# Second attention pass of a hybrid backbone block: one subtraction of the maps for both heads of a step

## The chip, the cores and the metric

The kernel runs on one core of a Trainium2 chip. The metric is the device time of one execution in microseconds; the median of three runs before the change is 3882.36 us (3880.23 to 3885.21).

## The reference

Two layers act on 2048 latent tokens and a prefix of 256 context tokens, each of width 1024. A layer normalises and modulates its input, projects it to 14 slices of 256 columns, runs four mixers side by side (a two-way RG-LRU, a two-way HGRN2, a Conformer convolution of 31 taps, differential attention), gates each with a SiLU, projects the concatenation back, normalises it and adds it, gated, to the stream. Everything is fp32. The change is in the attention. It has 4 heads, each with two softmax maps over the keys (2304 of them for a latent query, 256 for a context query):

```
s = einsum('bqhd,bkhd->bhqk', q, keys) * scale        # 8 maps, d = 32
p = softmax(s, axis=-1).reshape(b, 4, 2, q, k)
a = p[:, :, 0] - lam * p[:, :, 1]                      # difference of the two maps
o = einsum('bhqk,bkhe->bqhe', a, vals)                 # e = 64
y = rms_norm(o, norm_g) * (1 - lam_init)
```

## The kernel before, in words

The instructions of the whole program are traced in Python and a scheduler then orders them engine by engine. It simulates the engines in time: among the instructions whose inputs and buffers are free it takes the one that was traced first. `mix` interleaves generators in given proportions and thereby sets the traced order; `issue_after` puts an instruction behind another one on the same engine. The order on each engine, the DMA queues of SP and ScalarE among them, is fixed in the program.

A layer has four stages. `half0` and `half1` project the tokens, and find the maximum and the sum of every row of the maps (first pass of attention). `first` and `second` make the second pass, which recomputes the scores with the row's maximum and logarithm of the sum folded in as two more rows of the contraction, so that one exponential gives the finished probabilities.

The second pass (`attention`, `att_b`) runs over two pairs of heads and, for each pair, over blocks of 512 queries (in layer 0 also one of the 256 context queries). A block is a chain of steps, one for each 128 keys: 18 steps for latent queries, 2 for the context block; 148 steps in layer 0 and 144 in layer 1. In a step each of the two heads has two score products into a two-bank accumulator `sb` (two such buffers), one exponential on ScalarE from there into `pb`, and one VectorE operation (`scalar_tensor_tensor`) that subtracts the second map, times lambda, from the first. `values` multiplies the differences of both heads with V and accumulates into `po`, a single buffer of one bank, head 0 in partitions 0 to 63 and head 1 in 64 to 127. Those products are held back in the list `late` and issued two steps later, behind the first head's score products. A product in fp32 appears as two records in the trace. After the last key `head_norm` squares `po` on ScalarE, multiplies `po` by the gate on VectorE (the gate's tile comes by DMA), sums the squares with TensorE, takes the reciprocal root on GpSimd, spreads it with TensorE, multiplies and stores.

Beside the steps run, in `first` (the first 92 steps), the second half of the RG-LRU (`lru`: long VectorE scans, stores issued from ScalarE), the splitting of the output weights and in layer 0 the modulation of layer 1; in `second` (the rest) the output projection (`out_rows`, 128 tokens at a time) and the convolution (`conf`, 30 VectorE operations for each of two channel tiles, begun in `first`). `out_rows` keeps its result in `ot` (two buffers), adds the residual from `xt` (one buffer) and stores from ScalarE's queue; `xt` and `y` are loaded on SP.

Of the kernel before, what the change touches and what calls it, by code (L numbers as in the profile page):

```python
# [97 lines left out]
class _Kern:  # L98
# [232 lines left out]
    def layer(self, l):  # L331
        tc, dr = self.tc, self.dr
        last = l == DEPTH - 1
        self.S = S = {}
        for n in ("hq", "hff", "hkf", "hfb", "hkb", "g0", "g1", "g2", "g3", "cv", "qh", "ql", "kh", "kl"):
            S[n] = dr.tile([GW, T], F32, name=f"{n}_{l}")
        for n in ("hv", "av"):
            S[n] = dr.tile([T, GW], F32, name=f"{n}_{l}")
        S["y"] = dr.tile([D, T], F32, name=f"y_{l}")
        for n in ("lab", "lub", "lyf"):  # L340
            S[n] = dr.tile([GW, 1024], F32, name=f"{n}_{l}")
        for n, w in (("cu", 3), ("cg", 30)):
            S[n] = dr.tile([GW, w + 1024], F32, name=f"{n}_{l}")
        if not last:
            S["xn"] = dr.tile([T, D], F32, name=f"xn_{l}")
        a, z = ("left", "right") if l % 2 == 0 else ("right", "left")

        def pool(es, name, bufs, side=None, **k):
            return es.enter_context(tc.tile_pool(name=f"{name}{l}", bufs=bufs, side=side, reuse_waits="tile", **k))

        self.pool = pool
        halo = ExitStack()
        self.hb = pool(halo, "hB", 1, a)
        self.st = pool(halo, "st", 4, a)
        self.wp = pool(halo, "w", 2, a)
        self.keep = pool(halo, "keep", 1, a)
        self.carry = {}
        self.tanhs = []
        self.pend = None
        self.ready = set()  # L360
        self.normed = set()
        self.att_done = False
        self.parts = {}
        self.late = []
        self.steps = 0
        self.exp = None
        self.nz = {}
        self.mzd = {}

        self.X = self.hb.tile([P, 2, 4, D], F32, name="h3")  # L370
        self.prep_in(l, 1, self.X[:, 0])
        self.prep_in(l, 0, self.X[:, 1])
        self.w0 = [self.weights(l, 8, 0), self.weights(l, 7, 0)]
        if l == 0:
            with ExitStack() as es:
                pl = es.enter_context(tc.tile_pool(name="mod0", bufs=1, side=z, reuse_waits="tile"))
                pp = es.enter_context(tc.tile_pool(name="modp", bufs=3, space=PSUM, side="left", reuse_waits="tile"))
                mix([[self.modulations(0, 512, pl, 4, lambda: pp.tile([P, 512], F32, name="mps")), 1]])
                self.derived = [self.params(k, pl) for k in range(self.depth)]
        self.pr = self.derived[l]  # L380
        with ExitStack() as es:
            self.hx = pool(es, "hX", 1, z)
            self.m = self.mc = pool(es, "m0", 6, z)
            self.gt = pool(es, "gt0", 1, z)
            self.pre = pool(es, "pre0", 1, a)
            self.pj = pool(es, "pj0", 3, "left", space=PSUM)
            self.pq = pool(es, "pq0", 2, "left", space=PSUM)
            self.psA = pool(es, "psA0", 3, "right", space=PSUM)
            self.half0(l)
        with ExitStack() as es:  # L390
            self.pc = pool(es, "pc", 1, z)
            self.ap_ = self.hg = pool(es, "hg", 1, z)
            self.pj = pool(es, "pj1", 1, "left", space=PSUM)
            self.pq = self.pj
            self.psA = pool(es, "psA1", 4, "right", space=PSUM)
            self.psm = pool(es, "psm", 3, "right", space=PSUM)
            self.psn = lambda: self.psm.tile([P, 512], F32, name="pm")
            self.half1(l)
        halo.close()
        with ExitStack() as at:  # L400
            self.ap_ = pool(at, "at", 1, z)
            self.psB = pool(at, "psB", 1, "right", space=PSUM)
            self.psA = pool(at, "psA2", 1, "right", space=PSUM)
            self.psn = lambda: self.psA.tile([P, 512], F32, name="sa")
            self.mc = pool(at, "mc", 4, a)
            self.st = pool(at, "st1", 1, a)
            with ExitStack() as es:
                self.m = pool(es, "m1", 9, a)
                self.keep = pool(es, "keep1", 2, a)
                self.pq = pool(es, "pq1", 2, "left", space=PSUM)  # L410
                self.psc = lambda: self.pq.tile([P, 512], F32, name="pj")
                self.side = a
                self.first(l)
            self.psc = self.psn
            self.second(l, a)
        for k in [k for k in self.dbg if k.endswith(f"_{l}")]:
            self.nc.sync.dma_start(out=self.dbg[k], in_=S[k[:-2]])
        if not last:
            self.xprev = S["xn"]
# [324 lines left out]
    def first(self, l):  # L744
# [26 lines left out]
        with ExitStack() as es:  # L771
            pl = self.pool(es, "wout", 2, self.side)
            parts.append([self.out_weights(l, pl), 92])
            if l + 1 < self.depth:
                pl = self.pool(es, "mod", 1, self.side)
                parts.append([self.modulations(l + 1, P, pl, 2, lambda: self.pq.tile([P, 512], F32, name="pj")), 92])
            mix(parts)

    def second(self, l, side):
        with ExitStack() as es:  # L780
            for t in self.tanhs[-12:]:
                es.enter_context(self.tc.issue_after(t.ins))
            self.nc.scalar.preload_act_table_set("natural_log_exp_and_others")
        mix([[self.att, 148 - 92], [self.outp(l, side), 60], [self.convs, 30]])

    def attention(self, l):
# [3 lines left out]
        for i, (hp, b) in enumerate(todo):  # L790
            if b == self.qbs[0]:
                kv = {c: self.att_keys(l, hp, c) for c in KEYS}
            qst = q
            if i + 1 < len(todo):
                q = self.att_q(l, *todo[i + 1])
            yield from self.att_b(l, hp, b, kv, qst)
        while self.late:
            self.late.pop(0)()
        self.att_done = True
        self.steps = 999  # L800

    def lru(self, l, ct, u):
        nc, S, hf = self.nc, self.S, self.hf
# [334 lines left out]
    def att_b(self, l, hp, b, kv, qst):  # L1138
# [7 lines left out]
        def values(kt, cbs):  # L1146
# [6 lines left out]
            if kt < nk - 1:  # L1153
                return
            keep = hp == 1 and b == self.qbs[-1]
            rs = self.head_norm(l, po, n, self.pr["dg"], S["g3"], hp, t0, 768, keep)
            if hp == 1:
                self.ready.add(b)
            if keep:
                self.last_y = rs  # L1160

        for kt, (kst, V, ki) in enumerate(tiles):
            cbs = []
            for h in range(2):
                ps = self.psB.tile([P, 2, 512], F32, name="sb", bufs=2)
                for m in range(2):
# [1 line left out]
                        ps[:, m, :n], kst[:98, 2 * h + m, ki * P : (ki + 1) * P], qst[2 * h + m][:98, :n],  # L1168
                        start=True, stop=True,
                    )  # L1170
                pb = ap_.tile([P, 2, 512], F32, name="pb", bufs=5)
                self.exp = nc.scalar.activation(out=pb[:, :, :n], in_=ps[:, :, :n], func=AF.Exp)  # L1172
                cb = pb[:, 1, :]
                nc.vector.scalar_tensor_tensor(  # L1174
                    out=cb[:, :n], in0=cb[:, :n], scalar=self.pr["nlam"], in1=pb[:, 0, :n],
                    op0=ALU.mult, op1=ALU.add,
                )
                cbs.append(cb)
                if h == 0 and len(self.late) > 1:
                    with self.tc.issue_after(qk.ins):  # L1180
                        self.late.pop(0)()
            self.late.append(lambda kt=kt, cbs=cbs: values(kt, cbs))
            self.steps += 1
            yield

    def head_norm(self, l, po, n, g, gate, ct, t0, yoff, keep=False):

        nc, S, ap_ = self.nc, self.S, self.ap_
        sq = ap_.tile([P, 512], F32, name="nn", bufs=2)
        nc.scalar.activation(out=sq[:, :n], in_=po[:, :n], func=AF.Square)  # L1190
        rs = ap_.tile([P, 512], F32, name="nn", bufs=2)
        nc.sync.dma_start(out=rs[:, :n], in_=gate[ct * P : (ct + 1) * P, t0 : t0 + n])
        nc.vector.scalar_tensor_tensor(  # L1193
            out=rs[:, :n], in0=po[:, :n], scalar=g, in1=rs[:, :n], op0=ALU.mult, op1=ALU.mult
        )
# [293 lines left out]
    def out_rows(self, l, wp, yp, pp, wh, wl):  # L1489
# [3 lines left out]
        for b in self.qbs:  # L1493
# [12 lines left out]
            for q in range(n // P):  # L1506
# [9 lines left out]
                )  # L1516
                xt = yp.tile([P, D], F32, name="xt", bufs=1)
                nc.sync.dma_start(out=xt, in_=self.xsrc(l, t0 // P + q))
                t = yp.tile([P, D], F32, name="ot")
                ss = yp.tile([P, D // 512], F32, name="oss")  # L1520
                pss = {}

# [37 lines left out]
                for h in range(1, D // 512):  # L1560
                    nc.gpsimd.tensor_tensor(out=ss[:, 0:1], in0=ss[:, 0:1], in1=ss[:, h : h + 1], op=ALU.add)
                self.rsqrt(ss[:, 0:1], ss[:, 0:1], self.mhalf[:, 0:1], 1.0 / D, EPS)
                nc.vector.scalar_tensor_tensor(out=t, in0=t, scalar=ss[:, 0:1], in1=xt, op0=ALU.mult, op1=ALU.add)
                j = t0 // P + q
                dst = self.out[(j - 2) * P : (j - 1) * P, :] if l == DEPTH - 1 else S["xn"][j * P : (j + 1) * P, :]
                nc.scalar.dma_start(out=dst, in_=t)


def host_arrays(inputs):
# [85 lines left out]
```

## Time and profile before

| what | us |
|---|---|
| median of 3 runs | 3882.36 |
| profiled execution | 3890.28 |
| its span, first to last instruction | 3888.5 |
| TensorE busy | 3520.9 (91%) |
| VectorE busy | 2704.3 (70%) |
| ScalarE busy | 2208.2 (57%) |
| GpSimd busy | 1017.5 (26%) |
| second pass of layer 0, from | 1288 |
| second pass of layer 1, from | 3200 |

The engines are named PE (TensorE; PEld is its loading of weights), DVE (VectorE), ACT (ScalarE), POOL (GpSimd) and SP, with a q behind the name for the engine's queue. A row gives the line of the kernel, the operation, the tile written and the tiles read, and the shape. In the timeline the first two numbers are the start and the time from the start to the end of so many instructions; in brackets stands how long the engine was idle before, and what released it. PEclk is the granted clock of TensorE as a share of 2.4 GHz.

### The profile page before, as it was taken

Reading aid. Unit: us, or ns where it says so; the run is one execution under the profiler, and the core shown is the slowest. Engines: PE = TensorE matmul, PEld = TensorE weight load, DVE = VectorE, ACT = ScalarE, POOL = GpSimd, SP = SyncE. Lnnn points to the kernel's source line nnn. Section 1 sums busy time; section 2 is a strip of 40 time slices with the busy share of each in tenths; the row PEclk is TensorE's granted clock in tenths of the full one; section 3 lists DMA queues with packets and bytes.
Section 4 is the critical chain, followed back from the end, with each engine's and each line's share of the span. In section 5 each row is a group of like instructions: output and inputs, shape, how many; then the busy total and the mean of one; then the engine's idle time right before and its main releaser. Section 6 shows DMA issues by size and latency. Waiting matters only on the chain. (4 is left out here: it accounts for less than half of the span.)

```text
span 3888.5 us, 61466 instructions
## 1 busy us (share of the span) xinstructions
PE 3520.9 (91%) x21140; PEld 2444.0 (63%) x21140; DVE 2704.3 (70%) x4579; ACT 2208.2 (57%) x4732; POOL 1017.5 (26%) x1588
## 2 busy tenths in 40 slices
PE   6799898999999969999988998889999987899998
PEld 4678676667778633465666686666767783335366
DVE  5967757777787476786448677477788847668852
ACT  3164644667787567645331636446678756775631
POOL 2412115433451220001124241154435305000010
PEclk9899999999899979899999999889999998899999
DMA  5645446433332765232346545365343347432133
GB/s 219 215 163 156 143 160 190 134 119 110 109 105 94 201 231 182 74 110 83 125 149 207 178 164 179 127 179 155 116 121 106 97 127 248 137 89 74 49 117 111
DMA packets 390447, 549.30 MB, mean 141 GB/s; under 512 B 78376, under 2 KB 232024, under 8 KB 390104
## 3 DMA queue, kind: packets, MB, share of 16 engines
q1 hardware_dynamic: 313320, 438.37, 36.6%
q10 hardware_dynamic: 76816, 107.00, 7.9%
q8 instruction: 168, 2.75, 0.3%
q14 instruction: 143, 1.17, 0.1%
HBM read 349.68 MB, written 195.56 MB: 140 GB/s over the span
## 5 line engine op out<-in xcount | busy, mean ns | idle before, releaser
L998 ACT ACTIVATE sa<-sa,nm 128x512 f32<-128x512 f32 (+1 forms) x1296 | 795.4, 614 | 499.8 <-DVE nm L997 470.3
L997 DVE TENSOR_REDUCE nm<-sa 128x1 f32<-128x512 f32 (+1 forms) x1296 | 788.4, 629 | 337.5 <-PE sa L996 332.3
L498 PE MATMUL pj<-h,wh 128*128 128x256 f32 (+1 forms) x3712 | 965.6, 347 | 36.1 <-ACT s L556 16.2
L498 PEld LDWEIGHTS pj<-h,wh 128*128 128x128 f32 x3712 | 661.0, 198 | 135.7 <-issue 17.4
L1172 ACT ACTIVATE pb<-sb 128x1024 f32<-128x1024 f32 x584 | 571.6, 1018 | 287.0 <-PE sb L1167 191.4
L498 PE MATMUL pj<-h,wl 128*128 128x256 f32 (+1 forms) x1856 | 638.8, 344 | 5.1 <-DMA wl<-wp 5.1
L1174 DVE SCALAR_TENSOR_TENSOR pb<-pb,lam 128x512 f32<-128x512 f32 x584 | 445.9, 772 | 244.8 <-ACT pb L1172 243.6
L1167 PE MATMUL sb<-qst,kst 98*128 98x512 f32 (+1 forms) x1168 | 406.2, 453 | 50.9 <-ACT pb L1172 36.0
L1167 PEld LDWEIGHTS sb<-qst,kst 98*128 98x128 f32 x1168 | 194.9, 197 | 324.0 <-ACT pb L1172 231.6
L1149 PE MATMUL po<-pb,V 128*64 128x512 f32 (+1 forms) x1168 | 376.6, 660 | 21.6 <-DVE nn L1193 20.4
L498 PEld LDWEIGHTS pj<-h,wl 128*128 128x128 f32 x1856 | 366.0, 197 | 47.3 <-DMA wl<-wp 5.7
L996 PE MATMUL sa<-k,q 96*128 96x512 f32 (+1 forms) x896 | 353.2, 434 | 33.1 <-ACT sa L998 27.7
L905 DVE SCALAR_TENSOR_TENSOR m<-m,cols 128x1280 f32<-128x1280 f32 (+1 forms) x240 | 373.6, 1558 | 7.5 <-ACT m L900 6.5
L498 PE MATMUL pj<-hx,wh 128*128 128x512 f32 x896 | 296.6, 403 | 8.8 <-ACT s L556 8.3
L998 ACT ACTIVATION_READ_ACCUMULATOR sa<-sa,nm 128x1 f32 x1296 | 257.3, 199 | 0.5
L133 POOL TENSOR_SCALAR wh<-w 128x1024 fp32r<-128x1024 f32 x56 | 72.4, 1292 | 613.1 <-PE pj L498 540.7
L996 PEld LDWEIGHTS sa<-k,q 96*128 96x128 f32 x896 | 161.9, 191 | 101.0 <-ACT sa L998 58.8
L148 POOL TENSOR_SCALAR rsq<-rsq 128x8 f32<-128x8 f32 (+2 forms) x45 | 16.4, 364 | 778.8 <-DVE rsq L1210 778.4
L498 PEld LDWEIGHTS pj<-hx,wh 128*128 128x128 f32 x896 | 168.2, 192 | 46.5 <-ACT s L556 9.0
L498 PE MATMUL pj<-hx,wl 128*128 128x512 f32 x448 | 180.0, 402 | 0.0
L133 POOL TENSOR_SCALAR mq<-Q 64x256 f32<-64x256 f32 x238 | 106.2, 447 | 281.0 <-PE pm L1453 164.4
L996 PE MATMUL sa<-h,xs 96*128 96x512 f32 (+1 forms) x384 | 154.2, 419 | 24.0 <-ACT sa L998 23.8
(286 smaller groups left out, 5618.1 us busy)
## 6 DMA issues: line engine op xcount, KB each, us to landing
w<-in_w_in_dram SPq DMA_DIRECT2D x56, 512.0 KB
wp<-wh SPq DMA_DIRECT2D x56, 512.0 KB
wp<-wl SPq DMA_DIRECT2D x56, 512.0 KB
wh<-wp SPq DMA_DIRECT2D x56, 512.0 KB
wl<-wp SPq DMA_DIRECT2D x56, 512.0 KB
ctab<-in_rope_dram SPq DMA_DIRECT2D x32, 512.0 KB
wmod<-in_w_mod_dram SPq DMA_DIRECT2D x32, 512.0 KB
wo<-wop SPq DMA_DIRECT2D x32, 512.0 KB
```

The lines of the kernel that those rows point to most:

```text
L133: self.nc.gpsimd.tensor_scalar(out=out, in0=in_, scalar1=1.0, scalar2=1.0, op0=ALU.mult, op1=ALU.mult)
L148: gp.tensor_scalar(out=ss, in0=ss, scalar1=scale, scalar2=eps, op0=ALU.mult, op1=ALU.add)
L498: nc.tensor.matmul(ps[:, :n], a[:, k, :], hT[:, part, k, o : o + n], start=(m == 0), stop=(m == 23))
L905: nc.vector.scalar_tensor_tensor(out=acc[:, :W], in0=vb[:, k : k + W], scalar=self.col(l, C_FW + 2 * k + ct), in1=acc[:, :W], op0=ALU.mult ...
L996: nc.tensor.matmul(ps[:, :kn], qst[s][:96, q * P : (q + 1) * P], kst[:96, s, :], start=True, stop=True)
L997: nc.vector.tensor_reduce(out=nm, in_=ps[:, :kn], axis=AX.X, op=ALU.max, negate=True)
L998: nc.scalar.activation(out=ps[:, :kn], in_=ps[:, :kn], func=AF.Exp, bias=nm, accum_out=zc)
L1149: nc.tensor.matmul(po[64 * h : 64 * h + 64, :n], V[:, ki, 64 * h : 64 * h + 64], cbs[h][:, :n], start=(kt == 0), stop=(kt == nk - 1), skip ...
L1167: qk = nc.tensor.matmul(ps[:, m, :n], kst[:98, 2 * h + m, ki * P : (ki + 1) * P], qst[2 * h + m][:98, :n], start=True, stop=True,)
L1172: self.exp = nc.scalar.activation(out=pb[:, :, :n], in_=ps[:, :, :n], func=AF.Exp)
L1174: nc.vector.scalar_tensor_tensor(out=cb[:, :n], in0=cb[:, :n], scalar=self.pr["nlam"], in1=pb[:, 0, :n], op0=ALU.mult, op1=ALU.add,)
```

## The change

A step's two heads get one tile `pb` for both (two heads, two maps, 512 queries), from a pool of its own in each stage, and one subtraction for both. In `first` there are five such tiles and the products with V lag three steps; in `second` there are three and the lag is two, as before. `first` issues all held-back products at its end (`flush`). `head_norm` of the attention copies `po` to SBUF on ScalarE, and VectorE reads the copy. In `out_rows` the last operation writes into `xt`, which is stored, and `ot` has one buffer.

```diff
@@ layer
             self.psc = self.psn
+            self.pb = pool(at, "pbs", 1, z)
             self.second(l, a)
@@ first
+            self.pb = self.pool(es, "pb", 1, self.side)
+            self.deep = 5, 2
             mix(parts)
+            self.flush()
@@ second
+        self.deep = 3, 1
         mix([[self.att, 148 - 92], [self.outp(l, side), 60], [self.convs, 30]])
@@ attention
+        self.flush()
+        self.att_done = True
+        self.steps = 999
+
+    def flush(self):
         while self.late:
             self.late.pop(0)()
-        self.att_done = True
-        self.steps = 999
@@ att_b
-            rs = self.head_norm(l, po, n, self.pr["dg"], S["g3"], hp, t0, 768, keep)
+            spare = ap_.tile([P, 512], F32, name="spare")
+            rs = self.head_norm(l, po, n, self.pr["dg"], S["g3"], hp, t0, 768, keep, spare)
...
         for kt, (kst, V, ki) in enumerate(tiles):
-            cbs = []
+            pb = self.pb.tile([P, 2, 2, 512], F32, name="pb", bufs=self.deep[0])
             for h in range(2):
...
-                pb = ap_.tile([P, 2, 512], F32, name="pb", bufs=5)
-                self.exp = nc.scalar.activation(out=pb[:, :, :n], in_=ps[:, :, :n], func=AF.Exp)
-                cb = pb[:, 1, :]
-                nc.vector.scalar_tensor_tensor(
-                    out=cb[:, :n], in0=cb[:, :n], scalar=self.pr["nlam"], in1=pb[:, 0, :n],
-                    op0=ALU.mult, op1=ALU.add,
-                )
-                cbs.append(cb)
-                if h == 0 and len(self.late) > 1:
+                self.exp = nc.scalar.activation(out=pb[:, h, :, :n], in_=ps[:, :, :n], func=AF.Exp)
+                if h == 0 and len(self.late) > self.deep[1]:
                     with self.tc.issue_after(qk.ins):
                         self.late.pop(0)()
-            self.late.append(lambda kt=kt, cbs=cbs: values(kt, cbs))
+            nc.vector.scalar_tensor_tensor(
+                out=pb[:, :, 1, :n], in0=pb[:, :, 1, :n], scalar=self.pr["nlam"], in1=pb[:, :, 0, :n],
+                op0=ALU.mult, op1=ALU.add,
+            )
+            self.late.append(lambda kt=kt, cbs=[pb[:, h, 1, :] for h in range(2)]: values(kt, cbs))
@@ head_norm
+        if spare is not None:
+            nc.scalar.activation(out=spare[:, :n], in_=po[:, :n], func=AF.Copy)
+            po = spare
         nc.vector.scalar_tensor_tensor(
             out=rs[:, :n], in0=po[:, :n], scalar=g, in1=rs[:, :n], op0=ALU.mult, op1=ALU.mult
         )
@@ out_rows
-                t = yp.tile([P, D], F32, name="ot")
+                t = yp.tile([P, D], F32, name="ot", bufs=1)
...
-                nc.vector.scalar_tensor_tensor(out=t, in0=t, scalar=ss[:, 0:1], in1=xt, op0=ALU.mult, op1=ALU.add)
+                nc.vector.scalar_tensor_tensor(out=xt, in0=t, scalar=ss[:, 0:1], in1=xt, op0=ALU.mult, op1=ALU.add)
...
-                nc.scalar.dma_start(out=dst, in_=t)
+                nc.scalar.dma_start(out=dst, in_=xt)
```

## Rows read from the trace of the kernel before

**Rows 1.** Page, busy us and share of the span of each engine.

```profile
PE 3520.9 (91%) x21140; PEld 2444.0 (63%) x21140; DVE 2704.3 (70%) x4579; ACT 2208.2 (57%) x4732; POOL 1017.5 (26%) x1588
```

**Rows 2.** 20 us windows: busy of PE, PEld, DVE, ACT, POOL; PEclk; DMA share; GB/s.

```profile
1380.00:1400.00 20.00, 4.51 (x21) 2.87 (x21) 13.74 (x13) 1.98 (x2) 8.74 (x10) 0.50 1.02 353
...
3290.00:3310.00 20.00, 7.34 (x17) 2.13 (x18) 17.75 (x15) 6.31 (x6) 8.18 (x5) 0.59 0.82 300
```

**Rows 3.** Timeline, plain steps: start, us, instructions, [idle before them].

```profile
1559.11 1.94 ACT L1172 ACTIVATE pb<-sb 128x1024 f32<-128x1024 f32 x2 [0.35 <-PE sb L1167]
...
1560.17 0.75 DVE L1174 SCALAR_TENSOR_TENSOR pb<-pb,lam 128x512 f32<-128x512 f32 x1 [0.62 <-ACT pb L1172]
...
1560.48 1.35 PE L1167 MATMUL sb<-qst,kst 98*128 98x512 f32 x4
...
1561.76 1.08 PE L1149 MATMUL po<-pb,V 128*64 128x512 f32 x4
...
1564.92 1.35 PE L1167 MATMUL sb<-qst,kst 98*128 98x512 f32 x4
```

**Rows 4.** Timeline, steps beside a convolution of layer 1.

```profile
3646.10 0.73 PE L1167 MATMUL sb<-qst,kst 98*128 98x512 f32 x2
3646.26 1.30 DVE L905 SCALAR_TENSOR_TENSOR m<-m,cols 128x1039 f32<-128x1039 f32 x1
...
3646.76 1.07 PE L1149 MATMUL po<-pb,V 128*64 128x512 f32 x2
...
3649.43 0.73 PE L1167 MATMUL sb<-qst,kst 98*128 98x512 f32 x2
```

**Rows 5.** Groups by line and shape: count, busy us, mean ns, idle before.

```profile
L1174 DVE SCALAR_TENSOR_TENSOR pb<-pb,lam 128x512 f32<-128x512 f32 x576 | 441.3, 774 | 244.7 <-ACT pb L1172 243.6
...
L905 DVE SCALAR_TENSOR_TENSOR m<-m,cols 128x1039 f32<-128x1039 f32 x120 | 155.3, 1295 | 1.9 <-ACT m L900 1.4
...
L1563 DVE SCALAR_TENSOR_TENSOR ot<-ot,oss,xt 128x1024 f32<-128x1024 f32 x34 | 43.6, 1283 | 10.0 <-POOL oss L149 10.0
```

**Rows 6.** Timeline of TensorE, products with V of one head: first, last of 72.

```profile
1331.99 1.07 PE L1149 MATMUL po<-pb,V 128*64 128x512 f32 x2
...
3714.36 1.07 PE L1149 MATMUL po<-pb,V 128*64 128x512 f32 x2
```

**Rows 7.** Timeline, the two gaps at the end of the LRU.

```profile
1390.86 0.79 PE L1167 MATMUL sb<-qst,kst 98*128 98x512 f32 x1 [8.29 <-DMA qst<-mzd]
...
1402.18 1.28 ACT L1172 ACT_TABLE_LOAD   x1 [19.93 <-DMA qst<-qh]
...
3300.88 3.57 PE L1149 MATMUL po<-pb,V 128*64 128x512 f32 x8 [11.37 <-DVE nn L1193]
...
3302.42 1.24 ACT L810 ACTIVATE m<-m,cols 128x1025 f32<-128x1025 f32 x1 [13.11 <-DMA y<-m]
```

**Rows 8.** Timeline, a block's end at 1572, and ScalarE's first and last wait.

```profile
1488.71 3.85 ACT L1172 ACTIVATE pb<-sb 128x1024 f32<-128x1024 f32 x4 [4.38 <-PE po L1149]
...
1571.94 0.60 ACT L1190 ACTIVATE nn<-po 128x512 f32<-128x512 f32 x1
...
1576.71 1.68 PE L1215 MATMUL sa<-ident,rsq 128*64 128x128 f32 x16 [1.55 <-POOL m L751]
...
1579.81 3.68 PE L1149 MATMUL po<-pb,V 128*64 128x512 f32 x8 [1.42 <-DVE nn L1193]
...
1581.81 1.94 ACT L1172 ACTIVATE pb<-sb 128x1024 f32<-128x1024 f32 x2 [7.43 <-PE po L1149]
...
3518.97 1.02 ACT L1172 ACTIVATE pb<-sb 128x1024 f32<-128x1024 f32 x1 [5.78 <-PE po L1149]
```

**Rows 9.** Timeline of the tail, DMA issues of the output rows.

```profile
3786.61 0.32 SPq L1518 DMA_DIRECT2D xt<-xn  x1
...
3793.47 0.37 SPq L1508 DMA_DIRECT2D y<-y  x1
...
3884.99 0.34 ACTq L1566 DMA_DIRECT2D out_dram<-ot  x1
```

More of the change, by code (lines that the diff above doesn't have):

```diff
@@ L1170, in att_b, with head_norm @@
                     )
-                pb = ap_.tile([P, 2, 512], F32, name="pb", bufs=5)
-                self.exp = nc.scalar.activation(out=pb[:, :, :n], in_=ps[:, :, :n], func=AF.Exp)
-                cb = pb[:, 1, :]
-                nc.vector.scalar_tensor_tensor(
-                    out=cb[:, :n], in0=cb[:, :n], scalar=self.pr["nlam"], in1=pb[:, 0, :n],
-                    op0=ALU.mult, op1=ALU.add,
-                )
-                cbs.append(cb)
-                if h == 0 and len(self.late) > 1:
+                self.exp = nc.scalar.activation(out=pb[:, h, :, :n], in_=ps[:, :, :n], func=AF.Exp)
+                if h == 0 and len(self.late) > self.deep[1]:
                     with self.tc.issue_after(qk.ins):
                         self.late.pop(0)()
-            self.late.append(lambda kt=kt, cbs=cbs: values(kt, cbs))
+            nc.vector.scalar_tensor_tensor(
[3 more added lines that the diff above has]
+            self.late.append(lambda kt=kt, cbs=[pb[:, h, 1, :] for h in range(2)]: values(kt, cbs))
             self.steps += 1
             yield
-    def head_norm(self, l, po, n, g, gate, ct, t0, yoff, keep=False):
+    def head_norm(self, l, po, n, g, gate, ct, t0, yoff, keep=False, spare=None):
         nc, S, ap_ = self.nc, self.S, self.ap_
```

## The prediction

> **What bounds the kernel now.** I read the busy line of the page first, then 20 us windows over the two second passes of attention (1288 to 1980 us in layer 0, 3200 to 3889 us in layer 1), then the timeline of a plain step, of a step beside a convolution, of a block's end and of the two gaps that the windows showed, and last the counts by line. TensorE is busy 91% of the span [rows 1], so time is won where TensorE stands still or spends more than the work needs. The windows show both second passes nearly full except near the end of the first LRU half, where TensorE works 4.51 and 7.34 us of 20 and its granted clock is 0.50 and 0.59, the 1.2 GHz level for most of the window [rows 2].
>
> A plain step (two heads, four score products, two exponentials, two differences, two products with V) takes 2.22 us: the score products start at 1560.48 and, two steps on, at 1564.92 [rows 3]. TensorE is the limit there, with ScalarE close behind (1.94 us of exponentials a step). What the reader has to see is the product with V. It shows as four records in 1.08 us when both heads come one behind the other: the heads write different halves of the partitions of `po` (64h to 64h+64) and run side by side. Beside a convolution [rows 4] the heads come apart, with score products between them, and each head's two records take 1.07 us by themselves. Such a step takes 3.33 us (3646.10 to 3649.43). A head alone thus costs as much as both together.
>
> **1. One difference for both heads.** Removed: 584 differences of 774 ns (576 whole ones are shown); added: 292 of twice the width, for which the 128x1024 operation of the same kind shows 1283 ns [rows 5]. VectorE gives back 292 x (2 x 774 - 1283) = 77 us. I count none of it directly, since VectorE is not what ends the steps; it helps the terms below. What counts is that both heads now become ready with one instruction and `values` issues them one behind the other, so the single products vanish. In the two second passes 72 rows of products hold a single head (29 in layer 0, 43 in layer 1; first and last in [rows 6]), which makes 36 split steps. 20 of them stand alone or beside the output projection: 20 x 1.07 = 21 us of TensorE. 16 lie in 3606 to 3690 us, beside the convolution. There a step can't fall to 2.22, because VectorE would owe a difference and about one convolution operation per step, 1.28 + 1.30 = 2.58 us [rows 4, 5]: 16 x (3.33 - 2.58) = 12 us. Together 33; I take 30, since some of the 20 will meet ScalarE. Ends: 12 (only the convolution stretch) and 36 x 1.07 = 38.
>
> The price is a later difference. Now the second head's exponential ends at 1560.08 (half of the 1.94 us pair from 1559.11), its difference starts at 1560.17 and the next products with V that could need it at 1561.76 [rows 3]. A merged one started at 1560.17 ends at 1561.45: 0.3 us are left. In the plain stretches that is enough; where VectorE has other work it isn't, and that is the fifth rival.
>
> A rule speaks against this edit: the Trainium skill (Perfetto Trace Analysis, Optimizing Scalar/DVE Operations) says that where ScalarE or VectorE is not saturated but makes other engines wait, cutting instructions smaller may let work finish sooner, and merging is for a saturated engine. VectorE is at 70% [rows 1], so by the rule the edit is in the wrong direction. The same section puts VectorE's fixed cost at about 60 ns per operation; the estimate from that figure would be 292 x 0.06 = 18 us given back instead of 77. The rows give 265 ns per merge, and the measurement decides; by the rule's advice the time is that of the fifth rival.
>
> **2. Deeper beside the LRU.** In `first` the products with V lag three steps instead of two and five pairs instead of five single maps are held; in `second` the lag stays two, with three pairs. This costs TensorE nothing, work only moves. It gives VectorE 2.2 us more before a late difference stops TensorE, which is about one scan. It has its effect in the two gaps at the LRU's end [rows 7]: in layer 1 TensorE stands 11.37 us for `po`, which waits for the head norm's multiplication behind the LRU's work on VectorE, while ScalarE's queue stands 13.11 us at the LRU's stores; in layer 0 it stands 8.29 us for a query load, and ScalarE 19.93 us. The stores are issued from ScalarE in order, in front of the next exponentials, so `po` alone doesn't open these gaps, and the query load is not touched. I take 8, about one lag step per gap and some of the 1.2 GHz time behind it. Ends: 33 (both ScalarE waits gone) and -10 (a new order of the queues makes a gap longer; nothing excludes it).
>
> The flush at the end of `first` brings the last differences onto the path: one exponential (0.97) and one merged difference (1.28), 2.3 us twice if nothing covers them. I take 5 as cost for this and all that follows, with ends 0 and 16.
>
> **3. Accumulators copied out by ScalarE.** At a block's end `po` (one buffer) is held until VectorE has multiplied it by the gate, and that operation waits for the gate's load. The row of the block at 1572 us [rows 8] shows all: square at 1571.94; TensorE waits 1.55 us for GpSimd, on which the reciprocal root runs (the row names the small operation behind it); then 1.42 us for VectorE's read of `po`; ScalarE has no free map and stands 7.43 us. Nine block ends in the stretches without output projection have such a wait of ScalarE, 4.38 to 7.43 us apart from one of 3.21, 52.4 us together (first and last in [rows 8]). With the copy, `po` is free after square and copy, 2 x 0.60 us of ScalarE. The copy itself is paid where ScalarE is close to the limit, 9 x 0.6 = 5 us; the other nine copies lie beside the output projection, where TensorE's work hides them. What is late next is the root: its chain on GpSimd isn't shortened, but the next block's products no longer have to stand behind it. I take 2.4 us per block end, 22 in all, between 0 (the root takes over the whole wait) and 52.4 - 5 = 47.
>
> **4. The output row in place.** `ot` has one buffer, the result goes into `xt`, and so the next load of `xt` waits for the store instead of the last operation. Behind it on SP is the next load of `y`. The store of a row takes 3.5 us (issued 3884.99, span end 3888.5). In the tail `xt` is issued at 3786.61 and `y` only at 3793.47, when its own buffer is free [rows 9]: the longer wait ends at 3790.1, in front of `y`. Hidden; without that cover 16 tail rows by up to 3.5 us would pay. One buffer of `ot` is free again some 3 us after a row's end, while the next row's first half needs 24 products. Nothing.
>
> **Sum.** 30 + 8 + 22 - 5 = 55 us. The profiled execution took 3890.28 us (span 3888.5), 7.9 us over the median of the runs, 3882.36; 3890.3 - 55 = 3835, and less 8 that is **3827 us** as measured.
>
> **Rivals** (times as measured).
> Second, *the block's wait only changes its name*: TensorE's queue keeps the root ahead of the next block's products, and `po` was not the last thing waited for. For it: at 1576.71 the root ends the first part of the wait. Against: the read of `po` ends the second part, and it is later. 30 + 8 - 5 = 33: 3849.
> Third, *the gaps close too*: all upper ends, 38 + 47 + 33 = 118: 3764. For it: with ten maps instead of five ScalarE can work ahead into the gap. Against: its queue is in order, and the stores stand in it.
> Fourth, *the pairs gain only what VectorE leaves*: single products vanish but TensorE then waits for exponentials, block ends as in the second rival, gaps as now: 12 - 5 = 7, so 3875, no change.
> Fifth, *the merged difference is late* (the other side): in `second` the lag is still two, and 120 convolution operations of 1.30 us (two channel tiles, 30 each, in each layer) [rows 5] share VectorE. One that starts just before an exponential ends makes the difference 1.30 late, of which 0.3 is covered; with 0.7 us on each of them TensorE loses 84. 55 - 84 = -29: 3911. It decides from 55 / 0.7 = 79 of the 120 operations on. Against it: a convolution operation that starts right behind a merged difference ends 2.58 us after that one's start, 0.4 us behind the next step's time.
>
> **Chances.** Forecast 0.45, second 0.21, third 0.15, fourth 0.10, fifth 0.09. A measurement of this kernel can tell 0.2%, 7.8 us, from no change, so the fourth counts as the same. Faster 0.81, same 0.10, slower 0.09. The range reaches from just above the third's time to beyond the fourth's: 3768 to 3880; the fifth and the outermost part of the third are left out.
>
> **What would show it.** Right: no row with two records of the product with V between score products; steps of about 2.6 us instead of 3.33 beside the convolution in layer 1; differences of 1.28 us, VectorE 70 to 80 us less busy; TensorE waits for ScalarE, no longer for VectorE, in front of a block's first product with V, and the nine waits of ScalarE sum to under 30 us. Wrong: single products still there; waits for the difference in front of products with V that sum to more than 20 us; the gaps at the LRU's end longer than now; `y` loads in the tail issued behind a wait for a store.

## The result and the profile after

The changed kernel takes 3836.77 us (median of 4 executions, 3828.5 to 3846.51), the kernel before beside it 3881.3; the ratio is 0.9886 (95% interval 0.9864 to 0.9907), so 44 us or 1.1% less. The forecast was 3827. The profiled execution took 3839.82 us, 50.5 less than the one of before.

The page of the kernel after, its span and busy line, answers to [rows 1]: VectorE is 64 us less busy (77 were forecast), TensorE 49.

```profile
span 3838.0 us, 61038 instructions
...
PE 3471.8 (90%) x21140; PEld 2426.5 (63%) x21140; DVE 2640.7 (69%) x4287; ACT 2211.1 (58%) x4750; POOL 1011.9 (26%) x1588
```

Groups by line of the kernel after: count, busy us, mean ns, then the idle time of the engine before them by what ended it. First ScalarE's exponentials, then the score products, the differences, the products with V and their weight loads.

```profile
L1180 ACT ACTIVATE pb<-sb 128x1024 f32<-128x1024 f32 x584 | 568.9, 1019 | 204.3 <-PE sb L1176 192.3 <-PE po L1157 3.5 <-DMA wo<-wop 3.4
L1176 PE MATMUL sb<-qst,kst 98*128 98x512 f32 (+1 forms) x1168 | 402.9, 454 | 58.9 <-ACT pb L1180 46.6 <-DMA qst<-mzd 9.6 <-DMA kst<-kh 1.4
L1185 DVE SCALAR_TENSOR_TENSOR pb<-pb,lam 128x1024 f32<-128x1024 f32 x292 | 381.2, 1307 | 225.0 <-ACT pb L1180 220.4 <-DMA V<-av 3.9
L1157 PE MATMUL po<-pb,V 128*64 128x512 f32 (+1 forms) x1168 | 327.1, 641 | 11.3 <-DVE pb L1185 10.7 <-ACT spare L1202 0.2
...
L1157 PEld LDWEIGHTS po<-pb,V 128*64 128x64 f32 x1168 | 59.9, 139 | 119.1 <-DVE pb L1185 58.1 <-issue 47.8 <-DVE m L913 4.4
```

The same four groups and the weight loads in the kernel before:

```profile
L1172 ACT ACTIVATE pb<-sb 128x1024 f32<-128x1024 f32 x584 | 571.6, 1018 | 287.0 <-PE sb L1167 191.4 <-PE po L1149 70.8 <-DMA wl<-wp 8.4
L1174 DVE SCALAR_TENSOR_TENSOR pb<-pb,lam 128x512 f32<-128x512 f32 x584 | 445.9, 772 | 244.8 <-ACT pb L1172 243.6
L1167 PE MATMUL sb<-qst,kst 98*128 98x512 f32 (+1 forms) x1168 | 406.2, 453 | 50.9 <-ACT pb L1172 36.0 <-DMA qst<-mzd 9.5 <-DMA qst<-qh 2.7
L1149 PE MATMUL po<-pb,V 128*64 128x512 f32 (+1 forms) x1168 | 376.6, 660 | 21.6 <-DVE nn L1193 20.4 <-DVE pb L1174 1.1
...
L1149 PEld LDWEIGHTS po<-pb,V 128*64 128x64 f32 x1168 | 71.8, 143 | 152.1 <-issue 102.7 <-DVE nn L1193 20.9 <-DVE pb L1174 19.2
```

A row of four records holds four score products (1168 records for 292 steps of four) but only two products with V, which show as two records each.

Two things are to be seen. The same 1168 products with V take 49.5 us less (376.6 to 327.1). And the waits have changed their names, not their sum: TensorE's 20.4 us behind the head norm (`nn`) are gone, but its waits for the difference went from 1.1 to 10.7 and those of the score products for an exponential from 36.0 to 46.6, together 20.2 more.

Timeline of the kernel after, steps beside a convolution of layer 1 and a block's end among them (answers to [rows 4, 8]; start and length in us).

```profile
3603.49 1.35 PE L1176 MATMUL sb<-qst,kst 98*128 98x512 f32 x4
...
3604.78 1.08 PE L1157 MATMUL po<-pb,V 128*64 128x512 f32 x4
3605.29 1.30 DVE L913 SCALAR_TENSOR_TENSOR m<-m,cols 128x1039 f32<-128x1039 f32 x1
3605.78 1.21 PE L1176 MATMUL sb<-qst,kst 98*128 98x512 f32 x4
...
3607.93 1.35 PE L1176 MATMUL sb<-qst,kst 98*128 98x512 f32 x4
...
3610.53 0.60 ACT L1197 ACTIVATE nn<-po 128x512 f32<-128x512 f32 x1
3611.00 0.62 ACT L1202 ACTIVATE spare<-po 128x512 f32<-128x512 f32 x1
...
3611.67 1.08 PE L1157 MATMUL po<-pb,V 128*64 128x512 f32 x4 [0.24 <-ACT spare L1202]
```

The products stand as four records again. Two steps take 4.44 us (3603.49 to 3607.93, 2.29 and 2.15), so 2.22 a step, as much as a plain one, instead of 3.33. At the block's end TensorE waits 0.24 us for the copy.

The windows at the LRU's end (answer to [rows 2]; busy of PE, PEld, DVE, ACT, POOL; clock): in layer 0 the gap is half open. In layer 1 everything comes earlier, and the emptiest window there is now 3240 to 3260 with 12.00 us of TensorE's work.

```profile
1380.00:1400.00 20.00, 8.90 (x31) 3.29 (x30) 16.30 (x16) 10.91 (x14) 2.53 (x4) 0.76 0.84 270
...
3240.00:3260.00 20.00, 12.00 (x50) 6.94 (x48) 13.37 (x11) 12.16 (x15) 15.24 (x14) 0.83 0.72 235
...
3280.00:3300.00 20.00, 18.64 (x73) 8.70 (x74) 17.41 (x15) 18.38 (x21) 7.75 (x7) 0.83 0.55 187
```

I divide the execution at three instructions that both kernels have: the last transpose of the row maxima in layer 0 (the second pass starts), the first transpose of `h` in layer 1, and the last transpose of the maxima there. Windows of the two second passes (busy us of PE, PEld, DVE, ACT, POOL; granted clock), before and then after:

```profile
1272.60:2008.80 736.20, 668.78 (x2971) 381.86 (x2968) 465.71 (x604) 398.48 (x493) 98.93 (x135) 0.94 0.45 141
3175.50:3888.50 713.00, 636.81 (x2519) 347.64 (x2516) 439.75 (x518) 380.44 (x457) 86.04 (x111) 0.93 0.39 121
```

```profile
1270.00:1988.50 718.50, 647.20 (x2971) 374.78 (x2968) 437.87 (x456) 400.41 (x503) 100.20 (x135) 0.95 0.46 144
3166.30:3838.00 671.70, 600.87 (x2444) 335.47 (x2441) 406.53 (x372) 380.65 (x464) 81.97 (x110) 0.94 0.41 128
```

The second passes are 17.7 and 41.3 us shorter. TensorE's busy time in them falls by 57.5 us (1305.6 to 1248.1); its idle time, window less busy, stays: 143.6 before, 142.1 after. The 50.5 us of the span are 17.7 + 41.3 + 2.6 (start) - 11.1: the first half of layer 1, in which nothing was edited, takes 1177.8 us (1988.5 to 3166.3) instead of 1166.7 (2008.8 to 3175.5).

### The profile page after: what moved, and what is told of

It reads as the page before. It is cut to its first block, busy times and chain, and to the rows that moved or that the text cites. A ratio compares the mean times of both kernels' runs of the same rounds, so it can differ in the third digit from the quotient of the medians.

```text
span 3838.0 us, 61038 instructions
## 1 busy us (share of the span) xinstructions
PE 3471.8 (90%) x21140; PEld 2426.5 (63%) x21140; DVE 2640.7 (69%) x4287; ACT 2211.1 (58%) x4750; POOL 1011.9 (26%) x1588
## 5 line engine op out<-in xcount | busy, mean ns | idle before, releaser
L1185 DVE SCALAR_TENSOR_TENSOR pb<-pb,lam 128x1024 f32<-128x1024 f32 x292 | 381.2, 1307 | 225.0 <-ACT pb L1180 220.4
L1176 PE MATMUL sb<-qst,kst 98*128 98x512 f32 (+1 forms) x1168 | 402.9, 454 | 58.9 <-ACT pb L1180 46.6
L1157 PE MATMUL po<-pb,V 128*64 128x512 f32 (+1 forms) x1168 | 327.1, 641 | 11.3 <-DVE pb L1185 10.7
```

Of the source, the lines that this page charges most:

```text
L1157: nc.tensor.matmul(po[64 * h : 64 * h + 64, :n], V[:, ki, 64 * h : 64 * h + 64], cbs[h][:, :n], start=(kt == 0), stop=(kt == nk - 1), skip ...
L1176: qk = nc.tensor.matmul(ps[:, m, :n], kst[:98, 2 * h + m, ki * P : (ki + 1) * P], qst[2 * h + m][:98, :n], start=True, stop=True,)
L1185: nc.vector.scalar_tensor_tensor(out=pb[:, :, 1, :n], in0=pb[:, :, 1, :n], scalar=self.pr["nlam"], in1=pb[:, :, 0, :n], op0=ALU.mult, op1= ...
```

## The experiments

The theory was that the parts act in different places and add up; the rival, that they depend on each other. The kernels of each group ran on one chip beside the kernel before.

**Row in place, both layers**, as in the change:

```diff
-                t = yp.tile([P, D], F32, name="ot")
+                t = yp.tile([P, D], F32, name="ot", bufs=1)
...
-  ...scalar_tensor_tensor(out=t, in0=t, ...);  nc.scalar.dma_start(out=dst, in_=t)
+  ...scalar_tensor_tensor(out=xt, in0=t, ...);  nc.scalar.dma_start(out=dst, in_=xt)
```

> The kernel before with the fourth part alone: one buffer for the output row's product, result written into xt and stored from there. Theory (the parts act in different places and their gains add): the store is over before the next load of y can start, so nothing, within 8 us of before (3881). Rival (the tail waits for the store): some of the 34 rows pay up to 3.5 us, time up by 10 to 60 us, and y loads stand behind the load of xt in the trace.

Measured: 3905.52, ratio 1.0042 (1.0025 to 1.0058): 16 us slower, inside the rival's range. But the rows of the tail follow each other every 12.4 us (12.45 before, from one `y` load to the next). The theory's number fell, and the rival's place isn't where the time went; the row in layer 1 alone, below, settles that.

**Merged difference alone** (with the row in place, for room):

```diff
-                pb = ap_.tile([P, 2, 512], F32, name="pb", bufs=5)      # one for each head
+            pb = ap_.tile([P, 2, 2, 512], F32, name="pb", bufs=3)       # one for both; one difference behind the heads
```

> The kernel before with one difference for both heads, three pairs held and a lag of two steps in both halves, and the output row in place (needed for room); no copy of the accumulator, no deeper tiles. Theory (gains add): the single products vanish and give 17 to 30 us, 3851 to 3864; the waits at the block ends stay near 52 us in sum; the gap at the end of layer 1's LRU half stays. Rival (the merged difference needs the depth and the copy): with a lag of two everywhere and the accumulator held, the later difference costs beside the LRU what the pairs give, within 8 us of before or slower.

Measured: 3858.99, ratio 0.9922 (0.99 to 0.9944). Against the row in place alone that is 0.9922 / 1.0042 = 0.988, 46 us (31 to 61 if both intervals lie at their worst): more than expected. The products with V, with the row in place alone and then with the merged difference, take 41.5 us less:

```profile
L1149 PE MATMUL po<-pb,V 128*64 128x512 f32 (+1 forms) x1168 | 380.4, 660 | 30.3 <-DVE nn L1193 25.7 <-DVE pb L1174 4.5
```

```profile
L1149 PE MATMUL po<-pb,V 128*64 128x512 f32 (+1 forms) x1168 | 338.9, 664 | 27.5 <-DVE nn L1191 16.1 <-DVE pb L1176 11.3
```

From this kernel to the whole change, that is with copy and depth added, the ratio goes from 0.9922 to 0.9886, 14 us; the two intervals overlap, so this isn't shown.

**Copy alone** (`spare`, the argument of `head_norm` and the ScalarE copy, on the kernel before):

> The kernel before with ScalarE's copy of the accumulator at block ends and nothing else. Theory (gains add): six plain block ends give back some 4 us each, 17 to 26 us in all, 3855 to 3864, and ScalarE no longer waits for products at block ends. Rival (the copy pays only together with the pair): with two differences a step the products come apart more often (some 160 single ones in the order of TensorE's queue instead of 76, at about 0.5 us for every further one), 85 x 0.5 = 40 us eat the gain: 3880 or slower.

Measured: 3892.35, ratio 1.0011 (0.9995 to 1.0026). The rival holds. Windows of its two second passes:

```profile
1262.10:2006.90 744.80, 691.58 (x2971) 382.01 (x2969) 469.90 (x604) 404.75 (x503) 102.19 (x135) 0.94 0.46 139
3187.00:3894.60 707.60, 640.76 (x2444) 339.09 (x2441) 437.03 (x516) 385.51 (x464) 82.47 (x110) 0.95 0.40 122
```

TensorE's idle time is 53.2 + 66.8 = 120.0 us, 23.6 less than before, almost the 22 of the forecast; its busy time is 1332.3, 26.8 more. In TensorE's timeline 149 rows of products hold two records, one head alone, instead of 72.

**Deeper tiles alone** (ten single maps and a lag of three in `first`, six and two in `second`, the flush; row in place for room):

```diff
-                pb = ap_.tile([P, 2, 512], F32, name="pb", bufs=5)
+                pb = self.pb.tile([P, 2, 512], F32, name="pb", bufs=2 * self.deep[0])
```

> The kernel before with the deeper tiles alone (ten single maps and a lag of three steps beside the LRU, six and two after it, the products issued to the last at the seam), and the output row in place for room. Theory (gains add): 3 to 16 us, nearly all at the end of layer 1's LRU half, where TensorE's 20 us windows near 3290 no longer fall to 7 us; 3865 to 3878. Rival (the gap closes because the accumulator comes free earlier, by the copy): nothing, within 8 us of before, the windows near 3290 as low as before.

Measured: 3909.91, ratio 1.0061 (1.0037 to 1.0084), of which the row in place accounts for 1.0042. Alone it gives nothing that can be told apart. The windows went the theory's way all the same: the emptiest near the end of layer 1's LRU half holds 12.87 us (3260 to 3280). But in layer 0 the head norm now keeps TensorE waiting where the kernel before has no such gap:

```profile
1649.49 2.83 PE L1157 MATMUL po<-pb,V 128*64 128x512 f32 x6 [20.85 <-DVE nn L1201]
```

**One layer at a time.** With the change in layer 1 only, TensorE's queue is the same as before, instruction by instruction, up to the second pass of layer 1.

```diff
+            yield from (self.att_b0, self.att_b1)[l](l, hp, b, kv, qst)   # old and new att_b; pool, flush, row by layer too
-            yield from self.att_b(l, hp, b, kv, qst)
```

> The whole change in layer 1 only; layer 0 as before. Every instruction up to the first score product of layer 1's second pass is then planned as before. Theory (layer 1's second pass gains some 53 us, 697 to 643 from its first exponential to the end, and the order of layer 1's first half, which comes out differently as soon as layer 0 is edited, gives some 20 back): 3829, between 3821 and 3837, at least as fast as the change in both layers; first half of layer 1 (first transpose to first exponential) near 1183 us. Rival (that half only scatters from execution to execution): it takes 1200 us here too, and layer 1's share of the gain is 26 to 35, 3847 to 3856.

> The whole change in layer 0 only; layer 1 as before. Theory (layer 0's second pass gains 18 us, the new order of layer 1's first half costs 20): within 8 us of before. Rival (scatter): 18 us faster than before, 0.995 of it.

Measured: layer 1 alone 3857.12, ratio 0.992 (0.9895 to 0.9945); layer 0 alone 3881.8, ratio 0.998 (0.9964 to 0.9996). Layer 0 alone came out as its theory had it, and the two layers add up to 31 + 8 = 39 of the 44 us. For layer 1 alone the expected 3829 was a miss; 31 us lie in the rival's range. From the first transpose to the first exponential, the stretch that the expectation named, layer 1's first half takes 1213 us there (1183 before, 1206 after), long as the rival had it; but 45 us of that are a late start of the second pass, treated below. Up to the last transpose of the maxima it takes 1168.0 us, not longer. Over all profiled executions that half (first transpose of `h` to last transpose of the maxima) takes:

| layer 0 as before, that half planned as before | us | layer 0 edited, that half planned anew | us |
|---|---|---|---|
| before | 1166.7 | after | 1177.8 |
| whole change in layer 1 | 1168.0 | row in place | 1176.4 |
| copy in layer 1 | 1170.8 | merged difference | 1180.9 |
| merged difference and copy in layer 1 | 1173.4 | copy | 1180.1 |
| two differences in layer 1 | 1161.2 | deeper tiles | 1174.1 |
| row in layer 1 | 1166.6 | whole change in layer 0 | 1179.7 |
| other end, layer 1 | 1169.4 | other end, both layers | 1176.2 |

The means are 1168.0 and 1177.9 and no value of one column lies among the other: scatter explains a few microseconds, editing layer 0 costs about 10. TensorE's order in that half differs from the kernel before's within its first 109 records in every kernel on the right, and in none on the left. That it is the new order, and not something else that layer 0 leaves behind, fits but wasn't separated; with the deeper tiles only 333 of some 7420 records stand in another place, and that half is 6 us longer all the same (1174.1 against the mean of 1168.0).

**Copy in layer 1 alone**, and **the change in layer 1 without its depth**:

> ScalarE's copy of the accumulator alone, in layer 1 alone. Theory (the copy takes idle time from TensorE but with two differences a step more products come apart, 106 single ones in the order of its queue instead of 76): TensorE's idle time in layer 1's second pass 10 to 25 us less than 76, its busy time 10 to 20 us more than 637; 0 to 10 us faster. Rival (the copy is worth its block ends by itself): busy time as before, 15 to 25 us faster.

> The change in layer 1 alone without its second part: three pairs and a lag of two steps in both halves, no flush at the seam; merged difference, copy and row in place as changed. Theory (the gap at the LRU's end closes by the copy; the depth gives nothing beside it): within 8 us of the whole change in layer 1. Rival (the depth closes the gap): 8 to 25 us slower than that, and TensorE's 20 us windows near the LRU's end fall to 7 to 12 us again.

Measured: 3887.23, ratio 0.9995 (0.9979 to 1.0011), and 3864.11, ratio 0.9946 (0.9928 to 0.9963). Layer 1's second pass with the copy alone has 62.9 us of idle time (711.30 less 648.41) for 76.2, and 11.6 us more busy time, as the theory had it:

```profile
3180.60:3891.90 711.30, 648.41 (x2519) 349.07 (x2517) 437.92 (x518) 386.21 (x465) 85.13 (x111) 0.95 0.40 121
```

Without the depth the kernel is 7 us behind the whole change in layer 1, but the two intervals overlap: what the depth is worth there stays open. The time lies in the theory's range; the emptiest window near the LRU's end (11.02 us, 3300 to 3320) in the rival's.

**Two differences, all else changed, in layer 1**:

```diff
-            nc.vector.scalar_tensor_tensor(out=pb[:, :, 1, :n], ..., in1=pb[:, :, 0, :n], ...)
+            for h in range(2):
+                nc.vector.scalar_tensor_tensor(out=pb[:, h, 1, :n], ..., in1=pb[:, h, 0, :n], ...)
```

> The whole change in layer 1 alone, but with two differences a step, one for each head. Theory (the single instruction is what keeps the two heads' products together): 77 single products in the order of TensorE's queue instead of 29, TensorE's busy time in layer 1's second pass back to 625 to 650 us from 608, and 15 to 30 us slower than the whole change in layer 1, near 3875. Rival (the depth and the copy carry the gain, or the pair tile alone does): within 8 us of the whole change in layer 1.

Measured: 3884.23, ratio 0.9997 (0.9987 to 1.0008). Copy, depth and pair tile without the single instruction are worth nothing. Groups of its second pass in layer 1, and then those of the whole change in layer 1:

```profile
L1238 DVE SCALAR_TENSOR_TENSOR pb<-pb,lam 128x512 f32<-128x512 f32 x288 | 221.9, 783 | 106.6 <-ACT pb L1232 105.6 <-DMA m<-cu 0.2
L1209 PE MATMUL po<-pb,V 128*64 128x512 f32 x576 | 193.0, 656 | 0.2 <-ACT spare L1255 0.2
```

```profile
L1237 DVE SCALAR_TENSOR_TENSOR pb<-pb,lam 128x1024 f32<-128x1024 f32 x144 | 193.8, 1348 | 104.2 <-ACT pb L1232 103.6
L1209 PE MATMUL po<-pb,V 128*64 128x512 f32 x576 | 164.7, 652 | 3.0 <-DVE pb L1237 2.8 <-ACT spare L1254 0.2
```

The products with V cost 28.3 us more, and TensorE's busy time in that window is 643.2 us against 608.3, as the theory had it. The products hardly wait (0.2 us, for the copy); they only keep TensorE busy longer. The single heads are back: in layer 1's second pass 46 rows of products hold two records, none with the whole change in layer 1. Three rows beside the convolution, with no idle time between them:

```profile
3612.76 1.07 PE L1209 MATMUL po<-pb,V 128*64 128x512 f32 x2
3613.76 0.73 PE L1228 MATMUL sb<-qst,kst 98*128 98x512 f32 x2
3614.42 1.07 PE L1209 MATMUL po<-pb,V 128*64 128x512 f32 x2
```

**Row in layer 1 alone**:

> The output row in place, in layer 1 alone. Theory (the 16 us that this part costs alone in both layers come from another order of the first half of layer 1, not from a wait in the tail): within 8 us of before. Rival (the row waits for its store): 8 to 16 us slower, and more idle time of TensorE behind VectorE's and ScalarE's work on a row in 3740 to 3890 us.

Measured: 3887.78, ratio 0.9999 (0.9983 to 1.0014). Nothing in its own place, as the prediction had it. In its tail `y` comes 4.1 us behind `xt` on SP, which has waited for the store, and the row after that in its usual 12.4 us:

```profile
3797.54 0.32 SPq L1570 DMA_DIRECT2D xt<-xn  x1
3801.60 0.37 SPq L1560 DMA_DIRECT2D y<-y  x1
3809.87 0.32 SPq L1570 DMA_DIRECT2D xt<-xn  x1
3813.98 0.37 SPq L1560 DMA_DIRECT2D y<-y  x1
```

**Deep pool from the other end of the memory.** The traces with depth showed a late start of the second pass.

```diff
-            self.pb = self.pool(es, "pb", 1, self.side)
+            self.pb = self.pool(es, "pb", 1, self.zs)    # the end from which the attention's own pool is taken
```

> The whole change in layer 1 alone, with the deep pool allocated from the other end of the memory, whose tiles are released before the second pass starts. Theory (the first exponential waits for memory that the projections still hold, 45 us after the last transpose instead of 16, and TensorE idles meanwhile): the first exponential again at about 16 us, 4 to 12 us faster than the whole change in layer 1. Rival (the LRU sets the end of this stretch and the late start costs nothing): the first exponential early too, but the time within 4 us.

> The changed kernel, both layers, with the deep pool allocated from the other end of the memory. Theory (late start in both layers): 8 to 24 us faster than the changed kernel, 0.983 to 0.987 of before. Rival (late start costs nothing): 0.987 to 0.990 of before, like the changed kernel.

Measured: layer 1 alone 3844.0, ratio 0.9896 (0.988 to 0.9913); both layers 3825.61, ratio 0.9864 (0.9846 to 0.9883). First exponential of layer 1's second pass, and the 50 us from the last transpose, of the whole change in layer 1 and then with the other end:

```profile
3209.35 0.37 ACT L626 COPY s<-pj 128x256 f32<-128x256 f32 x1 [3.08 <-PE pj L500]
3209.62 1.03 ACT L1232 ACTIVATE pb<-sb 128x1024 f32<-128x1024 f32 x1
...
3164.40:3214.40 50.00, 37.59 (x257) 33.77 (x254) 4.13 (x7) 7.32 (x12) 1.32 (x4) 0.91 0.83 201
```

```profile
3194.46 1.02 ACT L1232 ACTIVATE pb<-sb 128x1024 f32<-128x1024 f32 x1 [6.03 <-PE sb L1228]
...
3176.10:3226.10 50.00, 43.84 (x284) 37.10 (x282) 9.81 (x11) 14.28 (x19) 1.31 (x4) 0.93 0.79 179
```

The first exponential comes 18 us after the last transpose instead of 45, and TensorE is busy 6.2 us more of the 50. This is the fastest version that ran, and it beats the kernel before; its interval overlaps that of the changed kernel, so that it beats that one too isn't shown. In the profiles of the kernels with both layers changed, layer 0's second pass gains (718.5 to 710.9) and layer 1's doesn't (671.7 to 675.0). That fits the starts: in the changed kernel the first exponential comes 43 us behind the last transpose in layer 0 and 28.5 us in layer 1, with the other end 17 and 24.

## Why the prediction was right, point by point

The total came out: 55 us forecast, 44 between the medians, 50.5 between the profiled executions. The measured 3837 lies midway between the forecast's 3827 and the second rival's 3849, so the time alone doesn't choose between them, and the composition was another. The first part was forecast at 30 and measured 46; copy and depth, less the cost of the flush, were forecast at 25 and add 14, not clear of noise; the row in place was forecast at nothing and costs 16. That these errors cancel to within 11 us is luck.

**One difference for both heads: mechanism right, term too small.** Forecast 30, measured 46 for both layers by the two kernels above, and 30 for layer 1 alone (0.992 against 0.9997), where 12 + some 6 had been counted. No row with two records is left [rows 6]. Two things were under-counted. The products lost 41.5 us of TensorE with the merged difference alone, more than the upper end of 36 x 1.07 = 38 (the further 12 us belong to the third part, below). And beside the convolution the step was held at 2.58 us for VectorE; it takes 2.22, since a convolution operation doesn't fall on every step (3601.24, 3605.29 and 3607.70 in the trace). The merged instruction itself takes 1307 ns where two took 1544: VectorE gives back 64 us, not 77.

The rule against this edit, that smaller instructions may finish sooner where VectorE isn't saturated (the Trainium skill, Perfetto Trace Analysis, Optimizing Scalar/DVE Operations), doesn't hold here: two instructions for one cost 30 us in layer 1 (16 to 44 if both intervals lie at their worst), with VectorE at 70% of the span in both kernels. What decides is the order they produce on TensorE. The Trainium skill (TensorEngine Tiling (Array Packing), Key Properties) says that different tiles of the array, here the column halves of the two heads, can load weights and multiply in parallel; the rows agree only for products that stand one behind the other in the queue (1.08 us for four records, 1.07 for two that stand alone).

**The sign called wrong did show.** Weight loads of the products wait 58.1 us for the difference, above the 20 that I had set (it was 19.2 before the change), the products themselves 10.7. The fifth rival, a late merged difference, is real in kind but cheap: of the loads' 58.1 us only 10.7 show as idle time in front of the products themselves.

**Deeper beside the LRU: not settled.** Forecast 8 less 5. Alone nothing; in layer 1, 7 us with overlapping intervals. What the prediction didn't have is the late start: the deep pool lies at the end of the memory where the projections' tiles still are, and the first exponentials stand behind the last of them. The layer 1 gap of 11.37 us [rows 7] is gone, but copy or depth alone closes it too, without a gain in time (the emptiest 20 us window there holds 12.9 us with the copy in layer 1 and with the deeper tiles, 3.5 before); the merged difference alone doesn't (a wait of 12.46 us for `nn`). The gap of layer 0 stays, 1.3 us longer for the same query load, a sign that had been called wrong (TensorE's timeline, after):

```profile
1401.16 1.19 PE L1176 MATMUL sb<-qst,kst 98*128 98x512 f32 x2 [9.55 <-DMA qst<-mzd]
```

**Accumulators copied out: the wait went as forecast, the gain didn't stay.** ScalarE's waits for `po` fell from 70.8 to 3.5 us, and the copy alone takes 23.6 us of idle time from TensorE, near the forecast's 22. But alone it costs as much busy time again, because the two heads' products come apart more often; in the changed kernel the idle time goes to the waits for differences and exponentials (20.4 us gone, 20.2 come). Why the earlier release draws them apart (the planner can place each head's product as soon as it is ready) is argued, not shown. This is the second rival in effect: the wait changed its name, though not to the one that it named.

What the prediction left out is the clock behind a block's end. In the kernel before, sixteen rows of products hold eight records (two steps), most of them behind the wait at a block's end; they take 2.7 us each in the mean, 43.7 together. The one at 1579.81 [rows 8] takes 3.68 us; TensorE has waited 1.55 and 1.42 us just before, and the granted clock is 0.50, the 1.2 GHz level. The merged difference alone still has fifteen such rows (43.1 us). The changed kernel has five, of 1.94 us each, at the full clock. The row and the clock of its stretch, before and then after:

```profile
1579.80:1583.50 3.70, 3.69 (x9) 0.85 (x9) 1.32 (x2) 1.69 (x2) 0.00 (x0) 0.50 0.19 71
```

```profile
1602.86 1.94 PE L1157 MATMUL po<-pb,V 128*64 128x512 f32 x8
...
1602.80:1604.80 2.00, 2.00 (x10) 0.56 (x9) 1.24 (x1) 1.64 (x2) 0.00 (x0) 1.00 0.28 90
```

So the last 12 us of the products (338.9 with the merged difference alone, 327.1 with everything) come with copy and depth and show as busy time, not as idle time; which of the two brings them wasn't separated.

**Row in place: right in its place, wrong for the kernel.** Nothing in layer 1 alone, 16 us in both layers. About 10 of these are the first half of layer 1, planned anew; the same 10 stand in the changed kernel. Another 8.5 are layer 1's second pass behind it (721.5 us against 713.0, and 712.9 with the row in layer 1 alone), where the gap at the LRU's end is 17.56 us instead of 11.37:

```profile
3313.94 3.68 PE L1149 MATMUL po<-pb,V 128*64 128x512 f32 x8 [17.56 <-DVE nn L1193]
```

The prediction had no term for work that it didn't see touched. With 10 us for it the sum would have been 45.

## What to carry to other kernels

Where two small products can run side by side, give them one producer, so that both become ready together: the gain is in the order on TensorE and is read from its busy time, not from waits. Test each part of a change alone and with the rest, and account busy and idle time separately: alone, the copy moved 24 us from one to the other and showed nothing. Behind a wait look at the granted clock too: here a row of eight records took 3.68 us at the 1.2 GHz level and 1.94 at the full clock. Under a planner that orders the whole program, price an edit at the end of the program, where nothing behind it can be planned anew, and keep some 10 us for what it does to the rest.

## What had not been expected

In all seven kernels that edit layer 0 (one of them layer 0 alone) the untouched first half of layer 1 is longer, about 10 us in the mean (1168.0 to 1177.9). And the end of the memory from which a pool is taken moved the first exponential by 27 us (45 to 18 us behind the last transpose), though the size of the pool was the same.
